# Projecting grouped q, k, v and memory's values with tokens on the rows, and a computed order for TensorE

## The chip, the cores and the metric

The kernel runs on one core of one Trainium2 chip. The metric is the device time of one execution in microseconds (us), the median of several runs. The core's engines are TensorE (PE; its weight loads are PEld), VectorE (DVE), ScalarE (ACT) and GpSimd (POOL); SyncE (SP) issues nearly all DMAs. 0.2% of the time before is 2.7 us.

## The reference

Two layers of an encoder over 512 tokens of width 1024, then a final RMSNorm. The token grid is 8 by 64; memory has 256 tokens.

```python
for l in range(2):
    h = rms_norm(x, norm_mix[l])
    na_q, na_k, na_v, g_q, g_k, g_v = split(h @ w_in[l])          # 512, 512, 512, 512, 128, 128 columns
    na = neighbourhood_attention(na_q, na_k, na_v, rpb)           # 8 heads of 64, a window of the grid
    g_q = rope(rms_norm_per_head(g_q)); g_k = rope(rms_norm_per_head(g_k))
    gqa = attention(g_q, g_k, g_v)                                # 8 q heads, 2 k/v heads, all 512 tokens
    x = x + concat(na, gqa) @ w_out[l]
    m = rms_norm(mem, norm_mem_kv[l])
    x = x + attention(rms_norm(x) @ w_mem_q, k(m), v(m)) @ w_mem_o   # 4 heads of 128
    u = conv3(rms_norm(x) @ w_up[l]) + conv_b                     # 2 x 2816 columns
    x = x + (silu(gate(u)) * val(u)) @ w_down[l]
return rms_norm(x)
```

## The kernel before

**Layout and precision.** x lies transposed, eight tiles `xT[c]` of 128 features by 512 tokens. Every float32 operand of a product is split into a rounded part `hi` and a rest `lo`, and a product is three matmuls, hi·hi, hi·lo and lo·hi, accumulated in PSUM (`mm3`; `gemm_T` runs it over chunks of 128 features). `Norm` holds the scaled operand (`xg`) and sums the squares.

**Weights.** `plan` lists the weight tiles in the order of use (`cols`, `plan_layer`, `plan_down`). `get_w` loads a tile through SP's queue into one of two `raw` buffers; `emit_split` (L647, L648) casts `hi` on ScalarE and subtracts `lo` on GpSimd (or VectorE), into one of four buffers. The last six tiles of the last down projection go into `r` tiles instead, which are held for both halves of the tokens.

**A layer.** Neighbourhood attention runs eight units (`na_scores` to `na_values`) woven with filler: `attn_fill` is a list of generators of projection work, a stretch of which is emitted between the steps of the units (`weave`, `NA_FILL`). The units project in `NA_ORDER`: q and k per pair of heads with the features on the rows (`project_qk`, 24 matmuls of 512 columns), v per four heads with the tokens on the rows, 256 columns at a time (`project_v`). The filler goes on with `gqa_project` in `GQA_ORDER`, out_na, the memory's keys and values (256 columns at a time) and the start of the output projection. Grouped attention follows in 16 units (`gqa_scores` to `gqa_values`), paced by `GQA_SLOT`.

**Grouped q, k, v before.** `gqa_project` makes one pair of heads, features on the rows, 512 tokens as columns. `gqa_rope` (L1255 to L1257) multiplies by the sine and cosine tables and squares; half-swapped rows are made by four DMAs; the sums of squares per head are four matmuls against `pairs` into a `tr` bank; k's inverse roots are spread over the rows by four matmuls against `ident`. `gqa_v` transposes v back with four TensorE transposes. Each step is put off by `late(n, ...)`, n times 3600 ns of TensorE time as the program counts it.

**Order.** The program is traced once; then `Order` plans the order of the instructions of ScalarE, VectorE and GpSimd with a model of their times (`due`, `run`), and fixes it by added dependencies. TensorE and SP keep the program's order (`InOrder.keep`, L69 and L82 are the lines of its wrappers, which all their instructions show).

**End.** `down_last` computes the last group of seven chunks for 256 tokens at a time, twice, and closes the final norm for each half (`Norm.stat`, `finish`).

Of the kernel before, what the change touches and what calls it, by code (L numbers as in the profile page):

```python
# [1 line left out]

# [29 lines left out]
GROUPS = [(0, 8), (8, 7), (15, 7)]  # L32
EPS = 1e-6
# [6 lines left out]
NA_ORDER = [("q", 0), ("k", 0), ("q", 1), ("k", 1), ("v", 0), ("q", 2), ("k", 2), ("q", 3), ("k", 3), ("v", 1)]  # L40
# [31 lines left out]
class Counted(InOrder):  # L72
# [4 lines left out]
    def matmul(self, out, lhsT, rhs, **k):  # L77
        n = 1
        for d in rhs.shape[1:]:
            n *= d  # L80
        self.ns += max(107.0, (n + 32) / 2.4)
        return self.keep(self.engine.matmul(out, lhsT, rhs, **k))  # L82


class Free:


    def __init__(self, engine):
        self.engine = engine

    def __getattr__(self, name):
        return getattr(self.engine, name)
# [110 lines left out]
ROUNDS = 16  # L203
# [102 lines left out]
class Order:  # L306

    FREE = ("ACT", "DVE", "POOL")  # L310

    def __init__(self, tc, kept):
# [10 lines left out]
        self.credit, best = {}, None  # L323
        for _ in range(ROUNDS):
            self.due()
            end, order, late = self.run()
            if best is None or end < best[0]:
                best = end, order
            for j, by in late:
                self.credit[j] = self.credit.get(j, 0.0) + by  # L330
# [80 lines left out]
    def run(self):  # L411
# [3 lines left out]
        ready, free_at = [0.0] * n, dict.fromkeys(HAND_OVER, 0.0)  # L415
# [9 lines left out]
        order, late, product = {e: [] for e in self.FREE}, [], None  # L425
# [3 lines left out]
        def earliest(j):  # L429
# [18 lines left out]
            return max(t, free_at[steps[j].engine])  # L448

        def choose(e):  # L450

            known = [(t, j) for j in open_[e] for t in [earliest(j)] if t is not None]
# [39 lines left out]
        def over_(s, t, end):  # L492

            for q in self.after[s.index]:
                need[q] -= 1
                begun = s.engine == "PE" == steps[q].engine or (s.index, q) in self.loose
                ready[q] = max(ready[q], t if begun else end + self.wait(s, steps[q]))
                if not need[q] and steps[q].engine in self.FREE:
# [7 lines left out]
        while len(issued) < n or moving:  # L506
            best = None
            for e in HAND_OVER:
                if e in self.FREE:
                    c = choose(e)  # L510
                elif at[e] < len(written[e]):
# [16 lines left out]
            if e in self.FREE:  # L528
                open_[e].remove(j)
                order[e].append(s)  # L530
            else:
                at[e] += 1
            if e == "PE":
                if product is not None and t > product + 150:
                    late.append((j, t - product))
# [9 lines left out]
            free_at[e] = t + s.busy  # L545
            issued.add(j)
            for name in s.names:
# [5 lines left out]
            if s.dma:  # L553
                if not moving:
                    clock = max(clock, t)
                moving.append([t + DMA_NS, s.bytes, j])
            else:
                over_(s, t, t + s.takes)
# [5 lines left out]
def encoder_kernel(ctx: ExitStack, tc: tile.TileContext, t: dict, out: bass.AP):  # L564
    nc = tc.nc
    kept = set()
    PE, SP = Counted(tc, nc.tensor, kept), InOrder(tc, nc.sync, kept)
# [65 lines left out]
    def emit_split(act=ACT, cuts=2):  # L633
# [6 lines left out]
        if eng[1:] == "r":  # L640
            hi, lo = rtile((nk, ncol)), rtile((nk, ncol))
        else:
            hi = wpool.tile([P, nk, ncol], F32R, tag="hi", name=nm("hi"))
            lo = wpool.tile([P, nk, ncol], F32R, tag="lo", name=nm("lo"))
# [6 lines left out]
    def get_w(key, ahead=AHEAD):  # L651
        n = done[0]
        assert plan[n][0] == key, (plan[n][0], key)
        ahead = n + 1 + ahead
        while ahead < min(len(plan), n + 1 + AHEAD_HELD) and plan[ahead][4][1:] == "r":
            ahead += 1
# [4 lines left out]
        while len(ready) < min(len(plan), ahead):  # L661
# [5 lines left out]
        else:  # L667
            load()
        done[0] += 1
# [12 lines left out]
    def plan_down(l, g):  # L682
        for m in range(KC):
            held = l + 1 == DEPTH and g + 1 == len(GROUPS) and m >= 2
            cols(("down", g, m), t["w_down"][l], *GROUPS[g], P * m, P, "Pr" if held else "P")

    def plan_memv(l, g):
        for kh in range(2):
            cols(("memv", g, kh), t["w_mem_kv"][l], 4 * kh, 4, 512 + 256 * g, 256)

    def plan_layer(l):
        w_in, w_out = t["w_in"][l], t["w_out"][l]
        for n, p in NA_ORDER:
# [6 lines left out]
        for n, g in enumerate(GQA_ORDER):  # L700
            c = {"k": 2048, "v": 2176}.get(g)
            cols(("g", g), w_in, 0, KC, 1536 + P * g if c is None else c, P)
        for mp in range(4):
            cols(("outn", mp), w_out, 0, 4, 256 * mp, 256, "P")
        for m in range(4):
            cols(("memk", m), t["w_mem_kv"][l], 0, KC, P * m, P)
        plan_memv(l, 0)
        for mp in range(4):
# [5 lines left out]
            if mp == 0:  # L714
                plan_memv(l, 1)
# [49 lines left out]
    qkg = cpool.tile([P, DEPTH, 2], F32, name="qkg")  # L765
# [4 lines left out]
    def load_parameters():  # L770
        SP.dma_start(par[:, 0, 8:], t["par"][:, 0, 8:])
        SP.dma_start(par[:, 1], t["par"][:, 1])
        SP.dma_start(qkg, t["qkg"])
# [4 lines left out]

    pairs = cpool.tile([P, 2], F32, name="pairs")
    nc.vector.memset(pairs, 0.0)  # L780
    for j in range(2):
        nc.vector.memset(pairs[64 * j : 64 * j + 64, j : j + 1], 1.0)
# [11 lines left out]
    def row_rep(rstd, n, tag, bufs, copy):  # L794

# [1017 lines left out]
```

## Time and profile before

| | |
|---|---|
| median of 3 runs | 1351.61 us (1350.64 to 1352.07) |
| the profiled execution | 1351.96 us |
| its span, first to last instruction | 1350.1 us |
| busy: PE, PEld, DVE, ACT, POOL | 1337.5, 1146.4, 902.1, 681.0, 698.8 us |
| instructions | 19133, of them 7018 matmuls |
| DMA | 139.88 MB, mean 104 GB/s |

Busy times of the engines overlap each other, and TensorE's overlap themselves: a matmul starts before its predecessor has drained, so a mean duration of one is longer than the step from one start to the next. A float32 matmul (against `ones`, `pairs`, `ident`) shows as two records. In rows of groups, the count stands behind x, and after the bar busy us, mean ns of one, and idle time of the engine before them with what ended it. The rows of waits give us in total, times, longest.

### The profile page before, as it was taken

The page shows a single profiled execution, that of the slowest core. Times are in us where ns is not written, and L with a number is a line of the kernel's source. Part 1 is how long each engine was busy: PE and PEld are TensorE (multiplying, and loading weights), DVE is VectorE, ACT ScalarE, POOL GpSimd, SP SyncE. Part 2 cuts the span into 40 slices and gives each one's busy share as a digit, 9 for nine tenths or more (in the row PEclk, how much of TensorE's full clock was granted, in tenths as well). Part 3 has the DMA queues.
Part 4 walks back from the last instruction along what each step waited for, and adds up shares of the span by engine and source line. Part 5 has one row for each costly group of instructions (what it writes and reads, how often), then busy time and mean ns, then how long its engine had stood idle before and what let it go on. Part 6 is the DMA issues. An engine that isn't in the chain of part 4 may idle for free.

```text
span 1350.1 us, 19133 instructions
## 1 busy us (share of the span) xinstructions
PE 1337.5 (99%) x7018; PEld 1146.4 (85%) x7018; DVE 902.1 (67%) x1598; ACT 681.0 (50%) x1258; POOL 698.8 (52%) x483
## 2 busy tenths in 40 slices
PE   9999999999999999999999999999999999999997
PEld 7898899888888888888898888988888888888887
DVE  6678874775984388178546678746769825862874
ACT  6776676564442244233557667855644423432441
POOL 2558766626444443443744576655554444444541
PEclk9999999999999999999999999999999999999999
DMA  7773222313333333332455531233233333333321
GB/s 217 201 190 109 79 63 73 116 45 96 96 103 98 94 94 94 109 94 82 127 155 164 140 106 49 79 95 94 63 94 98 104 94 94 93 95 109 90 83 63
DMA packets 219214, 139.88 MB, mean 104 GB/s; under 512 B 6000, under 2 KB 212080, under 8 KB 219120
## 3 DMA queue, kind: packets, MB, share of 16 engines
q1 hardware_dynamic: 218432, 138.13, 35.4%
q8 instruction: 56, 0.92, 0.3%
q10 hardware_dynamic: 688, 0.52, 0.1%
q14 instruction: 38, 0.31, 0.1%
HBM read 126.05 MB, written 2.10 MB: 95 GB/s over the span
## 4 chain that ended last, share of the span: by engine, by line
PE 93%; DVE 2%; DMA 1%; issue 1%; ACT 1%; POOL 1%; SPq 0%; DVEq 0%; POOLq 0%; ACTq 0%
PE mm L82 81%; PE sc L82 7%; PE tr L69 4%; PE tr L82 1%; DMA raw<-in_w_down 1%; POOL r L648 1%; DMA xT<-in_xT 0%; DVE t L846 0%; DMA raw<-in_w_in 0%; ACT r L1075 0%; SPq L69 0%; DVE r L875 0%; ACT hi L647 0%; ACT t L1257 0%; DVE r L1684 0%
## 5 line engine op out<-in xcount | busy, mean ns | idle before, releaser
L648 POOL TENSOR_TENSOR lo<-raw,hi 128x1024 fp32r<-128x1024 f32 (+2 forms) x268 | 511.5, 1919 | 498.6 <-ACT hi L647 494.7
L82 PE MATMUL mm<-xg,hi 128*128 128x512 f32 x1920 | 595.0, 391 | 0.0
L82 PEld LDWEIGHTS mm<-xg,hi 128*128 128x128 f32 x1920 | 356.1, 188 | 70.9
L647 ACT CAST hi<-raw 128x512 fp32r<-128x512 f32 (+2 forms) x276 | 226.3, 839 | 318.8 <-PE mm L82 267.8
L82 PE MATMUL mm<-xg,lo 128*128 128x512 f32 x960 | 373.9, 389 | 0.0
L82 PE MATMUL mm<-r,hi 128*128 128x512 f32 (+1 forms) x1096 | 316.3, 372 | 0.6 <-DVE r L1641 0.5
L1635 DVE SCALAR_TENSOR_TENSOR t<-t,par,t 128x7 f32<-128x7 f32 (+1 forms) x352 | 251.2, 773 | 25.0 <-ACT t L1628 25.0
L82 PEld LDWEIGHTS mm<-r,hi 128*128 128x128 f32 x1096 | 198.6, 189 | 35.6 <-DVE r L1641 0.7
L82 PEld LDWEIGHTS mm<-xg,lo 128*128 128x128 f32 x960 | 180.2, 188 | 37.9
L82 PE MATMUL mm<-r,lo 128*128 128x512 f32 (+1 forms) x548 | 203.6, 372 | 0.0
L82 PEld LDWEIGHTS mm<-r,lo 128*128 128x128 f32 x548 | 103.3, 188 | 17.9
L881 POOL TENSOR_SCALAR t<-t,s 128x512 f32<-128x512 f32 (+1 forms) x112 | 67.9, 622 | 75.0 <-DVE s L1323 36.1
L1620 DVE TENSOR_TENSOR t<-mm,rep 128x512 f32<-128x512 f32 x88 | 60.0, 686 | 63.0 <-PE mm L82 47.3
L1664 DVE TENSOR_TENSOR xT<-xT,mm 128x512 f32<-128x512 f32 x32 | 22.0, 686 | 104.5 <-PE mm L82 104.5
L1640 ACT CAST r<-t 128x512 fp32r<-128x512 f32 x44 | 27.3, 620 | 101.7 <-DVE t L1638 101.7
L1638 DVE TENSOR_TENSOR t<-t,t 128x512 f32<-128x512 f32 x44 | 68.2, 1551 | 4.3 <-ACT t L1637 0.5
L82 PE MATMUL sc<-r,r 128*128 128x256 f32 (+1 forms) x352 | 70.7, 333 | 0.3 <-DVE r L1081 0.3
L1628 ACT ACTIVATE t<-t,par 128x512 f32<-128x512 f32 x88 | 67.0, 806 | 1.2 <-DVE t L1620 1.2
L1317 ACT ACTIVATE t<-sc,s,qr 128x512 f32<-128x512 f32 x64 | 49.3, 775 | 32.2 <-DVE s L881 32.2
L82 PE MATMUL mm<-r,r 128*128 128x256 f32 (+1 forms) x428 | 62.5, 297 | 1.7 <-POOL r L648 1.1
L69 PE MATMUL tr<-ident,t 128*128 128x128 f32 x456 | 61.0, 273 | 0.7 <-DVE s L1267 0.7
L82 PEld LDWEIGHTS mm<-r,r 128*128 128x128 f32 x428 | 56.4, 191 | 5.0 <-POOL r L648 1.3
(160 smaller groups left out, 1607.8 us busy)
## 6 DMA issues: line engine op xcount, KB each, us to landing
raw<-in_w_up SPq DMA_DIRECT2D x88, 512.0 KB, 3.8
raw<-in_w_in SPq DMA_DIRECT2D x33, 512.0 KB, 4.1
raw<-in_w_down SPq DMA_DIRECT2D x32, 448.0 KB, 3.7
raw<-in_w_mem_kv SPq DMA_DIRECT2D x16, 512.0 KB, 3.8
raw<-in_w_down SPq DMA_DIRECT2D x16, 512.0 KB, 4.0
r<-in_bias SPq DMA_DIRECT2D x16, 384.0 KB, 4.9
r<-r SPq DMA_DIRECT2D x22, 256.0 KB, 5.6
raw<-in_w_out SPq DMA_DIRECT2D x8, 512.0 KB, 3.7
```

The lines of the kernel that those rows point to most:

```text
L69: return lambda *a, **k: self.keep(op(*a, **k))
L82: return self.keep(self.engine.matmul(out, lhsT, rhs, **k))
L647: act.copy(hi[:, k], raw[:, k])
L648: (POOL if eng[0] == "P" else DVE).tensor_sub(lo[:, k], raw[:, k], f(hi)[:, k])
L881: eng.tensor_scalar(e, e, sums[:, col : col + 1], 1.0, op0=ALU.mult, op1=ALU.mult)
L1317: ACT.activation(e, sc[j], AF.Exp, bias=nmx[:, c], scale=qrs[i][:, col : col + 1], accum_out=sums[:, c])
L1620: DVE.tensor_mul(u, us[side], ffn.rep)
L1628: ACT.activation(cc, u, AF.Identity, bias=par[:, l, CB + ch : CB + ch + 1], scale=w[1])
L1635: DVE.scalar_tensor_tensor(cc[:, dst], u[:, src], wi, cc[:, dst], op0=ALU.mult, op1=ALU.add)
L1638: DVE.tensor_mul(cs[0], cs[0], cs[1])
L1640: ACT.copy(acts[j][0], cs[0])
L1664: DVE.tensor_add(xT[m], xT[m], pm)
```

## The change

- Grouped q (`gq`) and grouped k and v together with the neighbourhood heads' second v (`kv`) are projected with the tokens on the rows, 512 columns of weights at a time, by `wide`; the memory's values too. `wide_cols` plans four weight tiles of two chunks by 512 columns for each.
- Rope is done with tokens on the rows: tables multiplied by the gains on GpSimd once a layer, the half swap as an addition of other columns on GpSimd, the sums of squares by VectorE reduces. The results are transposed by TensorE, four transposes per block of tokens for q and four for k. `gq` now holds blocks of tokens instead of pairs of heads.
- The filler's order changes: all grouped projections come in `NA_ORDER`, then the memory's values, out_na, two of the memory's keys; the other two keys go between the output rows.
- `Order` plans TensorE's order too, over the next 240 products that are not issued, replays each plan with spread times, and asks for 100 ns of margin at the operands that come from other engines.
- The last down group is split into four chunks for all 512 tokens and three chunks for each half; the final gain is applied on ScalarE, the last two squares are summed on TensorE, and the final multiplies take two chunks at a time.
- In layer 0's first k the second `lo` copy is made by GpSimd.

The diff, cut to its core:

```diff
-NA_ORDER = [("q", 0), ("k", 0), ("q", 1), ("k", 1), ("v", 0), ("q", 2), ("k", 2), ("q", 3), ("k", 3), ("v", 1)]
+NA_ORDER = [("q", 0), ("k", 0), ("q", 1), ("k", 1), ("v", 0), ("q", 2), ("k", 2), ("q", 3), ("k", 3), ("kv", 1), ("gq", 0)]
...
-GQA_ORDER = ["k", 0, 1, "v", 2, 3]
-NA_FILL = 2430
+NA_FILL = [[2800] * 6 + [1500] * 4, [2800] * 6 + [1400] * 4]
...
+TABLES = 1
 LATE = 3600
-N_RAW, N_W, N_R, N_T, N_S, AHEAD, AHEAD_HELD, N_WARM, N_LATE, N_FIRST = 2, 4, 21, 14, 24, 2, 5, 7, 4, (8, 16)
+N_RAW, N_W, N_R, N_T, N_S, AHEAD, N_WARM, N_FIRST = 2, 4, 21, 14, 24, 2, 7, (12, 24)
...
-class Counted(InOrder):
+class Free:
...
-        return self.keep(self.engine.matmul(out, lhsT, rhs, **k))
...
+        return self.engine.matmul(out, lhsT, rhs, **k)
...
+ROUNDS, REPLAYS, MARGIN, SHARES, STRETCH, SEED = 16, 2, 100.0, (0.0, 0.0, 0.5, 1.0, 2.0), 250, 0
+DMA_SPREAD = 1900.0, 3100.0
+AHEAD_MOST, PATIENCE = 240, 60.0
...
+    ORDERED = FREE + ("PE",)
...
+            for i in range(REPLAYS):
+                e, _, more = self.run(order, random.Random(i))
+                end, late = end + e, late + more
...
+        def product_next():
+            mine, i, seen, best = written["PE"], at["PE"], 0, None
+            while i < len(mine) and seen < AHEAD_MOST:
+                j = mine[i]
+                i += 1
+                if j in issued:
+                    continue
+                seen += 1
+                t = earliest(j)
+                if t is not None and (best is None or t < best[0] - PATIENCE):
+                    best = t, j
+                if best is not None and best[0] <= free_at["PE"] + PATIENCE:
+                    break
+            return best
...
+                short = MARGIN - (t - possible(j, fed))
+                if product is not None and short > 0:
+                    late.append((j, t - product, t - product + short))
...
-    PE, SP = Counted(tc, nc.tensor, kept), InOrder(tc, nc.sync, kept)
+    PE, SP = Counted(nc.tensor), InOrder(tc, nc.sync, kept)
...
+        if (l, g) == (DEPTH - 1, len(GROUPS) - 1):
+            for i, rows in enumerate(LAST):
+                for mp in range(4):
+                    cols(("down", "ab"[i], mp), t["w_down"][l], *rows, 256 * mp, 256)
+            return
         for m in range(KC):
-            held = l + 1 == DEPTH and g + 1 == len(GROUPS) and m >= 2
-            cols(("down", g, m), t["w_down"][l], *GROUPS[g], P * m, P, "Pr" if held else "P")
-    def plan_memv(l, g):
-        for kh in range(2):
-            cols(("memv", g, kh), t["w_mem_kv"][l], 4 * kh, 4, 512 + 256 * g, 256)
+            cols(("down", g, m), t["w_down"][l], *GROUPS[g], P * m, P)
...
+    def wide_cols(key, w, *slices):
+        for i in range(4):
+            loads, c = [], 0
+            for a, b in slices:
+                loads.append((lambda r, c=slice(c, c + b - a): r[:, :, c],
+                              w[2 * i * P : 2 * (i + 1) * P, a:b].rearrange("(k p) c -> p k c", p=P)))
+                c += b - a
+            plan.append(((key, i), loads, 2, 512, "P"))
...
+            elif n == "kv":
+                wide_cols(n, w_in, (1280, 1536), (2048, 2304))
+            elif n == "gq":
+                wide_cols(n, w_in, (1536, 2048))
...
+        wide_cols("memv", t["w_mem_kv"][l], (512, 1024))
...
-            DVE.tensor_scalar(part, sums(self.acc), 1.0 / D, EPS, op0=ALU.mult, op1=ALU.add)
-            warm()
-            DVE.scalar_tensor_tensor(v, sums(self.last), 1.0 / D, part, op0=ALU.mult, op1=ALU.add)
+            DVE.tensor_scalar(part, sums(self.acc, self.last[0]), 1.0 / D, EPS, op0=ALU.mult, op1=ALU.add)
+            DVE.scalar_tensor_tensor(v, sums(self.last[1]), 1.0 / D, part, op0=ALU.mult, op1=ALU.add)
...
-                    DVE.tensor_sub(k[o, 1], pm[r], f(k[r, 0]))
+                    POOL.tensor_copy(k[o, 1], k[r, 1])
...
+        def wide(key, blocks, ops, evict):
+            w, pms = [], {}
+            order = [(0, 0), (0, 1), (1, 0), (0, 2), (1, 1), (0, 3), (1, 2), (1, 3)]
+            order += [(b, i) for b in range(2, blocks) for i in range(4)]
+            for b, i in order:
+                if i == 0:
+                    pms[b] = ps_mm()
+                if i == len(w):
+                    w.append(get_w((key, i), min(AHEAD, N_W - 1 - i)))
+                bs = slice(b * P, b * P + P)
+                for k in (2 * i, 2 * i + 1):
+                    mm3(pms[b], ops[k][0][:, bs], ops[k][1][:, bs], *(v[:, k % 2] for v in w[i]), k == 0, k == KC - 1)
+                if b == blocks - 1 and i < AHEAD:
+                    prepare_w(i + 1)
+                if i == 3:
+                    evict(b, pms.pop(b))
+                yield
...
+        def project_kv(g):
+            vs = v_blocks(g)
+            gvt.append(rtile((NB, 2, P)))
+            gkt = [tmp() for _ in range(3)]
+            def evict(b, pm):
+                split_v(vblk[g][P * b], pm[:, 0:256], b)
+                split_v(gvt[0][:, b], pm[:, 384:512], b)
+                turn_by(1, pm[:, 256:384], b, *(v[:, b * P : b * P + P] for v in gkt))
+                if b == NB - 1:
+                    late(1, lambda: straddle(g, vs))
+                    late(1, lambda: gqa_k(*gkt))
+            yield from wide("kv", NB, xg, evict)
...
+        def gqa_tables():
+            rope, gains, tab = tmp((2 * NB, HD)), tmp((2, HD)), rtile((2, 2 * NB, HD), F32)
+            SP.dma_start(rope, t["rope"])
+            SP.dma_start(gains, t["qkg"][:, l])
+            for i in range(2):
+                POOL.tensor_tensor(tab[:, i], rope, gains[:, i].unsqueeze(1).to_broadcast([P, 2 * NB, HD]), op=ALU.mult)
+                gtab.append(tab[:, i].rearrange("p (t b) d -> p t b d", t=2))
...
-        def gqa_project(g):
...
+        def turn_by(i, pm, b, xs, cc, sq):
+            n = pm.shape[1] // HD
+            for v, tab in ((xs, gtab[i][:, 1, b]), (cc, gtab[i][:, 0, b])):
+                DVE.tensor_mul(by_head(v), by_head(pm), tab.unsqueeze(1).to_broadcast([P, n, HD]))
+            ACT.activation(sq, pm, AF.Square)
+        def rotate(xs, cc):
+            xs, cc = by_head(xs), by_head(cc)
+            halves = [slice(0, HD // 2), slice(HD // 2, HD)]
+            for a, b in (halves, halves[::-1]):
+                POOL.tensor_add(cc[:, :, a], cc[:, :, a], xs[:, :, b])
+        def transposed(cc):
+            tr = ps_t()
+            for c in range(4):
+                PE.transpose(tr[:, c * P : (c + 1) * P], cc[:, c * P : (c + 1) * P], ident)
+            return tr
...
+        def gqa_k(xs, cc, sq):
+            n = 2 * NB
+            ss, v, r = small(n), small(n), small(n)
+            DVE.tensor_reduce(ss, by_head(sq), axis=AX.X, op=ALU.add)
+            DVE.scalar_tensor_tensor(
+                v.rearrange("p (b j) -> p b j", j=2), ss.rearrange("p (b j) -> p b j", j=2), 1.0 / HD,
+                geps[:, 0].unsqueeze(2).to_broadcast([P, NB, 2]), op0=ALU.mult, op1=ALU.add)
+            POOL.tensor_tensor(r, v, mhalf[:, :n], op=ALU.pow)
+            rotate(xs, cc)
+            POOL.tensor_tensor(by_head(cc), by_head(cc), r.unsqueeze(2).to_broadcast([P, n, HD]), op=ALU.mult)
...
-        def gqa_rope(g, pm):
...
+        def project_gq():
+            yield from wide("gq", NB, xg, gqa_q)
+        def gqa_q(b, pm):
+            xs, cc, sq = tmp(), tmp(), tmp()
+            turn_by(0, pm, b, xs, cc, sq)
+            def norm():
+                ss, v = small(2 * NB), small(2 * NB)
+                DVE.tensor_reduce(ss, by_head(sq), axis=AX.X, op=ALU.add)
+                DVE.tensor_scalar(v, ss, geps[:, 1, b : b + 1], 1.0, op0=ALU.add, op1=ALU.mult)
+                POOL.tensor_tensor(qrs[b], v, mhalf[:, : 2 * NB], op=ALU.pow)
+                rotate(xs, cc)
+                late(1, turn)
+            def turn():
+                gq[b] = rtile((2, S))
+                split_q(transposed(cc), gq[b])
+            late(1, norm)
...
+            qs = slice(i * P, i * P + P)
+            assert gq[b] is not None and gk in whole_k
             sc = [ps_s() for _ in range(2)]
             for j in range(2):
                 for part in range(2):
-                    PE.matmul(sc[j], gq[i][:, j, qs], gk[j][:, part], start=part == 0, stop=part == 1)
+                    PE.matmul(sc[j], gq[b][:, j, qs], gk[j][:, part], start=part == 0, stop=part == 1)
...
+        def memory_values():
+            yield lambda: len(mops) == KC
+            memv.extend(rpair() for _ in range(MB))
+            yield from wide("memv", MB, mops, lambda b, pm: split_psum(*memv[b], pm, mem_rstd[:, b : b + 1]))
...
+        project = {"v": project_v, "kv": project_kv, "gq": lambda p: project_gq()}
...
-            PE, late, *([project_first(), *units[3:]] if l == 0 else units), *[gqa_project(g) for g in GQA_ORDER],
-            out_na(), memory_keys(), memory_values(0),
+            PE, late, *([project_first(), *units[3:]] if l == 0 else units),
+            memory_values(), out_na(), memory_keys(range(2)),
             close_rows(2, PartsView(parts, 4), lambda k: whole[k], lambda: nns.append(Norm(G_MQ, l)) or nns[0],
-                       memory_values(1)))
+                       memory_keys(range(2, 4))))
...
-            if s == 3:
-                gtab.append(rtile((2, S), F32))
-                SP.dma_start(gtab[0], t["rope"])
-                gqa_eps()
-            return [NA_FILL] * 3
+            if s == TABLES:
+                gqa_tables()
+            return [NA_FILL[l][s]] * 3
...
+        def down_last():
+            parts = [[acts.pop(j) for j in range(j0, j0 + nj)] for j0, nj in LAST]
+            ws = {}
+            def product(pm, i, m, ops):
+                if (i, m // 2) not in ws:
+                    ws[i, m // 2] = get_w(("down", "ab"[i], m // 2))
+                gemm_T(pm, ws[i, m // 2], ops, range(len(ops)), 0, len(ops) - 1, slice(P * (m % 2), P * (m % 2) + P))
+            for m in range(KC):
+                pm = ps_mm()
+                product(pm, 0, m, parts[0])
+                DVE.tensor_add(xT[m], xT[m], pm)
+            def finish(norm, y, last=False):
+                pr = row_bank(norm.rstd, NB // 2)
+                rep = tmp((256,))
+                ACT.copy(rep, (row_bank(norm.rstd, NB // 2) if last else pr)[:, :256])
+                for k in (0, 2, 6, 4):
+                    eng, by = (DVE, pr) if last and k < 6 else (POOL, rep)
+                    v = y[k // 4][:, k % 4 : k % 4 + 2]
+                    eng.tensor_mul(v, v, by[:, :256].unsqueeze(1).to_broadcast([P, 2, 256]))
+                for i, k in enumerate((0, 2, 4, 6)):
                     (ACT_IN_ORDER if last and i % 2 else SP).dma_start(
-                        out[k * P : (k + n) * P, norm.cols].rearrange("(k p) n -> p k n", p=P), y[k // 4][:, k % 4 : k % 4 + n])
-            norms = []
+                        out[k * P : (k + 2) * P, norm.cols].rearrange("(k p) n -> p k n", p=P), y[k // 4][:, k % 4 : k % 4 + 2])
+            norms, ys = [], []
             for half in range(2):
                 cs = slice(256 * half, 256 * half + 256)
-                hops = [(hi[:, cs], lo[:, cs]) for hi, lo in ops]
+                hops = [(hi[:, cs], lo[:, cs]) for hi, lo in parts[1]]
                 norms.append(Norm(cols=cs))
-                rows = []
+                ys.append([rtile((4, 256), F32) for _ in range(2)])
                 for m in range(KC):
-                    if half == 0:
-                        ws.append(get_w(("down", g, m)))
-                    rows.append(ps_mm()[:, :256])
-                    late = half == 0 and m < N_LATE
-                    gemm_T(rows[m], ws[m], hops, range(nj - 1 if late else nj), 0, nj - 1)
-                    for i in [m] if not late else range(N_LATE) if m == N_LATE - 1 else []:
-                        if late:
-                            gemm_T(rows[i], ws[i], hops, [nj - 1], 0, nj - 1)
-                        DVE.tensor_add(xT[i][:, cs], xT[i][:, cs], rows[i])
-                        norms[half].square(i)
-                        scale(half, i)
+                    pm = ps_mm()[:, :256]
+                    product(pm, 1, m, hops)
+                    DVE.tensor_add(xT[m][:, cs], xT[m][:, cs], pm)
+                    norms[half].square(m)
+                    ACT.activation(ys[half][m // 4][:, m % 4], xT[m][:, cs], AF.Copy, scale=gfin[:, m : m + 1])
```

More of the change, by code (lines that the diff above doesn't have):

```diff
@@ L447, in earliest @@
                 t = max(t, sorted(slots[k])[c - 1])
-            return max(t, free_at[steps[j].engine])
+            return t
+        def earliest(j):
+            t = possible(j, ready)
+            return t if t is None else max(t, free_at[steps[j].engine])
         def choose(e):
+            if given is not None:
+                if len(order[e]) == len(given[e]):
+                    return None
+                j = given[e][len(order[e])].index
+                t = earliest(j)
+                return None if t is None else (t, j)
             known = [(t, j) for j in open_[e] for t in [earliest(j)] if t is not None]
@@ L462, in choose @@
                     return t, q
-            return soon, j
+            if e == "POOL":
+                for q in open_["DVE"]:
+                    if steps[q].two_from_sbuf() and self.latest[q] < self.latest[j]:
+                        t = earliest(q)
+                        if t is not None and soon < t + 1 < soon + busy and soon + busy > self.latest[q]:
+                            t += steps[q].busy
+                            if t <= self.latest[j]:
+                                return max(t, soon), j
+            return soon, j
+        def product_next():
[6 more added lines that the diff above has]
+                seen += 1
+                t = earliest(j)
+                if t is not None and (best is None or t < best[0] - PATIENCE):
[3 more added lines that the diff above has]
+            return best
         def transfers(until):
@@ L497, in over_ @@
                 ready[q] = max(ready[q], t if begun else end + self.wait(s, steps[q]))
+                if s.engine != "PE":
+                    fed[q] = max(fed[q], end + self.wait(s, steps[q]))
                 if not need[q] and steps[q].engine in self.FREE:
@@ L544, in run @@
                 shared["DVE"] = t + s.busy
-            free_at[e] = t + s.busy
+            slow = 1.0 if draw is None or e not in self.FREE else 1.0 + 0.04 * draw.random()
+            free_at[e] = t + s.busy * slow
             issued.add(j)
+            while e == "PE" and at[e] < len(written[e]) and written[e][at[e]] in issued:
+                at[e] += 1
             for name in s.names:
@@ L639, in emit_split @@
             cuts = 1
[L640 to L644, printed above, removed]
+        hi = wpool.tile([P, nk, ncol], F32R, tag="hi", name=nm("hi"))
+        lo = wpool.tile([P, nk, ncol], F32R, tag="lo", name=nm("lo"))
         for i in range(cuts):
@@ L649, in emit_split, with prepare_w @@
         ready.append((hi, lo))
[L651 to L656, printed above, removed]
+    def prepare_w(ahead):
         def load():
@@ L850, in stat, with sums @@
             nb = self.n // P
-            def sums(sq):
+            def sums(*sqs):
                 pv = ps_t()
                 for b in range(nb):
-                    PE.matmul(pv[:, b : b + 1], sq[:, b * P : b * P + P], ones, start=True, stop=True)
+                    for i, sq in enumerate(sqs):
+                        PE.matmul(pv[:, b : b + 1], sq[:, b * P : b * P + P], ones, start=i == 0, stop=i == len(sqs) - 1)
                 return pv[:, 0:nb]
-            if self.last is None:
+            if not self.last:
                 self.rstd, self.var = rsqrt(sums(self.acc), nb, 1.0 / D, factor)
@@ L1793 @@
         "rope": _rope_tables(),
[L1794 removed]
+        "qkg": np.tile(np.stack([a[n][:, order] for n in ("gqa_q_norm", "gqa_k_norm")], axis=1), (P, 1, 1, 1)),
     }
```

240 lines of the change are left out of this document (82 added, 158 removed).

## The prediction

> **What bounds the kernel now.** I read the page first (busy shares, chain), then the chain in order of time, then TensorE's groups with shapes kept apart, then its waits, and last the windows of the attention stages.
>
> ```profile
> span 1350.1 us, 19133 instructions
> PE 1337.5 (99%) x7018; PEld 1146.4 (85%) x7018; DVE 902.1 (67%) x1598; ACT 681.0 (50%) x1258; POOL 698.8 (52%) x483
> PEclk9999999999999999999999999999999999999999
> PE 93%; DVE 2%; DMA 1%; issue 1%; ACT 1%; POOL 1%; SPq 0%; DVEq 0%; POOLq 0%; ACTq 0%
> ```
>
> TensorE is on 93% of the chain at full clock; the next engine, VectorE, is busy 67%. But a busy PE may still be stretched by short waits, so I price its work by the steps between starts. Two stretches of the chain have nothing but one shape:
>
> ```profile
> 328.00 342.76 PE mm L82 x1512
> 1330.01 10.07 PE mm L82 x84
> ```
>
> The first is layer 0's feed-forward part, all 512 columns: 342.76 / 1512 = 0.2267 us a matmul. The second is the end of the kernel, 256 columns: 10.07 / 84 = 0.1199 us. Two halves therefore cost 13.1 ns more than one whole. The small forms come from the order of time: eight transposes 83.82 to 84.65, so 0.104 each; eight records on `pairs` (four matmuls, two records each) 100.06 to 100.87, 0.81; eight on `ident,t` 110.05 to 110.94, 0.89.
>
> ```profile
> 83.82 1.07 PE L69 MATMUL tr<-ident,t 128*128 128x128 f32 x8
> 84.65 0.36 PE L82 MATMUL mm<-hi,xg 128*128 128x256 f32 x1
> ...
> 100.06 0.95 PE L82 MATMUL tr<-pairs,t 128*128 128x2 f32 x8
> 100.87 0.37 PE L82 MATMUL mm<-r,r 128*128 128x256 f32 x1
> ...
> 110.05 1.14 PE L82 MATMUL mm<-ident,t 128*128 128x128 f32 x8
> 110.94 0.48 PE L82 MATMUL mm<-xg,hi 128*128 128x512 f32 x1
> ...
> 164.82 1.17 PE L82 MATMUL sc<-r,r 128*128 128x512 f32 x4
> 165.82 0.64 PE L82 MATMUL mm<-xg,r 128*128 128x256 f32 x4
> ```
>
> The last pair shows a stall that no wait is listed for: four 512-column score products take 1.00 us, not 4 x 0.2267 = 0.91. About 0.09 us goes where a product's operand has only just come.
>
> Groups by shape (count, then busy and mean; busy overlaps, so I use the counts; first and last row of each width):
>
> ```profile
> L82 PE MATMUL mm<-xg,hi 128*128 128x512 f32 x1920 | 595.0, 391 | 0.0
> ...
> L69 PE MATMUL tr<-ident,t 128*128 128x128 f32 x456 | 61.0, 273 | 0.7 <-DVE s L1267 0.7
> L82 PE MATMUL mm<-r,r 128*128 128x256 f32 x380 | 49.5, 284 | 1.6 <-POOL r L648 1.1 <-ACT t L1257 0.5
> ...
> L82 PE MATMUL mm<-lo,r 128*128 128x256 f32 x64 | 18.1, 283 | 0.0
> ...
> L82 PE MATMUL sc<-xg,lo 128*128 128x512 f32 x32 | 12.3, 390 | 0.0
> L82 PE MATMUL tr<-pairs,t 128*128 128x2 f32 x80 | 9.5, 240 | 0.0
> L82 PE MATMUL tr<-ones,t 128*128 128x1 f32 x64 | 7.8, 241 | 0.2 <-DVE t L846 0.2
> ...
> L82 PE MATMUL mm<-ident,t 128*128 128x128 f32 x16 | 2.2, 280 | 0.0
> ```
>
> The ten 512-column groups hold 4616 matmuls (x 0.2267 = 1046.4), the nine of 256 columns 1712 (205.3), the transposes 47.4, `pairs` and `ones` some 15, the other small ones about 6: 1320 us of work. The span less about 4.5 us ahead of the first product and 6.7 us behind the last is 1339. So about 19 us of TensorE's time is stalls, and everything else is work: what the change takes off the work comes off the time, unless a new wait takes its place.
>
> ```profile
> PE mm L82 <- POOL r L648: 1.1, 1, 1.1
> PE mm L82 <- DVE r L1096: 0.7, 1, 0.7
> PE tr L69 <- DVE s L1267: 0.7, 1, 0.7
> PE mm L82 <- ACT t L1257: 0.5, 1, 0.5
> PE mm L82 <- DVE r L1641: 0.5, 1, 0.5
> PE sc L82 <- DVE r L1081: 0.3, 1, 0.3
> ```
>
> **The change, part by part** (TensorE's time over both layers).
>
> *Rope's sums.* The sums of squares per head no longer run on TensorE against `pairs`; VectorE reduces with tokens on the rows. Five projections a layer, ten groups of 0.81: -8.1 us. This is the largest term. The k rows spread through `ident` go too: two groups of 0.89, -1.8.
>
> *Transposes.* Grouped q needs four per block of tokens (16 a layer), k still 4 as new ones, and v's 4 go: 16 more a layer, 32 x 0.104 = +3.3.
>
> *Merged columns.* Values of heads 4-7 (96 halves a layer) together with grouped k and v (48 wholes) become 96 wholes: 48 merges a layer. Memory's values, 96 halves, become 48 wholes: 48 merges. The last down group, 336 halves, becomes 96 wholes and 144 halves: 96 merges. 288 x 13.1 ns = -3.8. The skill's page "TensorE: Matmul & The Clock Gate" (Back-to-back issue gap) speaks against this term: it gives the isolated gap as columns / 2.4 plus 2.5 ns, by which a merge is worth 2.5 ns, and the Trainium skill's sum for the 288 would be an estimated -0.7. The two stretches of one shape quoted above differ by 13.1 ns in this very kernel, so the trace disagrees and I stay with -3.8.
>
> *Closing sums.* In the last norm the sums of two squares are added on TensorE: four more small records in the first half, at about 0.1 each +0.4; the second half's lie under VectorE's work on the last row.
>
> Work in sum: -8.1 - 1.8 + 3.3 - 3.8 + 0.4 = **-10.0**.
>
> *The last down group* split 4 + 3. Its first products need the activations of columns 15-18 only, so the wait for the last one (L1641, 0.5) is covered by 8 x 12 x 0.2267 = 21.8 us, and the weights pass the ordinary buffers, at 5.4 us of products a tile, instead of six held ones (L648, 1.1). With 0.1-0.17 us of restart at each: **-2.1**. Late next is none: the last tiles' lo parts have the 5.4 us each.
>
> *The tail.*
>
> ```profile
> 1341.99 0.71 POOL s L867
> 1342.74 0.72 PE tr L82 x4
> 1343.46 0.02 issue
> ...
> 1343.56 0.38 ACT rep L801
> 1343.94 0.02 issue
> 1343.97 0.42 DVE r L1684
> ```
>
> VectorE's final multiplies stand behind ScalarE's copy of the same bank. With a second bank for the copy they can start near 1343.5; three pieces of 512 columns take as long as six of 256. **-0.4**, bounded by 0 (GpSimd's part ends last) and -0.5 (1343.97 to 1343.46).
>
> *Start.* For layer 0's first k, GpSimd copies what VectorE subtracted twice (L1081, L1096), and TensorE gets four more pieces of filler ahead of the first scores: of 0.7 + 0.3 and two restarts I take **-1.0**.
>
> *Moved to other engines.* Costed at nothing on TensorE's path, hidden by this slack:
>
> ```profile
> 100.00:130.00 30.00, 30.00 (x177) 26.24 (x177) 25.02 (x51) 20.49 (x51) 24.46 (x22) 1.00 0.38 109
> ...
> 175.00:215.00 40.00, 40.00 (x298) 37.33 (x297) 30.04 (x73) 31.17 (x73) 26.23 (x31) 1.00 0.22 66
> ```
>
> (columns: window, length, then PE, PEld, DVE, ACT, POOL busy.) VectorE per layer: five reduces come, close to this one's 682 ns, the subtractions of q get cheaper since they read PSUM, k's and v's multiplies go, four small pairs for kv come: about +1 us. GpSimd:
>
> ```profile
> L1278 POOL TENSOR_TENSOR t<-t,t 128x512 f32<-128x512 f32 x10 | 14.3, 1428 | 0.0
> L1272 POOL TENSOR_TENSOR qr<-s,mhalf 128x8 f32<-128x8 f32 x8 | 14.3, 1784 | 1.6 <-DVE s L1267 1.6
> ...
> L1314 DVE TENSOR_REDUCE s<-sc 128x1 f32<-128x512 f32 x64 | 42.0, 682 | 1.7 <-PE sc L82 1.5
> ```
>
> two table products and k's scaling at 1.43 each, less a copy, +4 us a layer; rotation in halves and powers as before. GpSimd's idle time in the 30 us shown is 5.5, so without that cover the weights' lo parts come up to 4 us late a layer.
>
> *SP's queue.* The four row-swap DMAs behind each rope go.
>
> ```profile
> SPq L69 <- DVE t L1255: 58.6, 10, 9.7
> ```
>
> SP stood 58.6 us behind them, weight loads queued after it; no PE wait names a load there, so I take 0. The tables' loads move from step 3 to step 1 of neighbourhood attention; the queue has weights and biases ahead of them, nothing waits for the tables before the first kv block. 0, bounded by -1 and +1.
>
> *TensorE's order computed.* Of 19.2 us of stalls, 2.1 and 1.0 are counted above, the tail's and the start's fixed part is about 3, leaving some 13, mostly restarts of 0.09. A product whose operand is not there can now be passed by a later one, and a product's feeders get 100 ns of margin. The wait on L1267 (0.7 and its restart) goes in any case with the `pairs` bank. But the order is planned on modelled times, and a bad guess is a new wait in a fixed order. Between -10 and +5, nearest the rows that name their cause, I take **-3.0**.
>
> Sum: -10.0 - 2.1 - 0.4 - 1.0 - 3.0 = -16.5; span 1350.1 to 1333.6. The profiled execution took 1351.96, 1.9 over its span; the runs' median 1351.61 is 0.35 below it. So 1333.6 + 1.86 - 0.35 = **1335.1**.
>
> **The rivals.**
>
> *The order takes nearly all of the stalls* (-10 instead of -3): 1328. For it: most are restarts a margin of 100 ns is meant for. Against: the restarts at the scores follow VectorE's and ScalarE's chains, which stay.
>
> *The order gains nothing*, and L1641 or L648 has a successor: 1335.1 + 3 to 5 = 1339.
>
> *The saved time turns into waits on other engines* in neighbourhood attention, where grouped q, k and v now all have to be projected. GpSimd at 24.46 of 30 speaks for it, ScalarE and VectorE at 78% and 75% in the window from 175 against. Then some 4.5 us a layer come back: 1344.
>
> *Slower: the door to grouped attention.* Before, its first scores needed one pair of q heads and k; two q projections came as filler later. Now its first four units need all four blocks of q, and k. From a block's last product: two multiplies and a reduce (2.1), the power (1.8), rotation (1.5), two deferrals of 3.6, transposes and splits (an estimate of 3 from two such multiplies and their ScalarE partners): about 15 us, covered by memory's values (48 x 0.2267 = 10.9) and three units. If that cover is used up too early, TensorE idles once a layer. At 9.6 us a layer (1335.1 + 19.2 = 1354.3) it decides for slower; the most, 15 uncovered, gives 1365.
>
> *No change*: a wait of 8 us a layer at the same door, 1351.
>
> **How the numbers follow.** Forecast (1331-1339) 0.50; order takes nearly all (below 1331) 0.16; order gains nothing (1339-1342) 0.14; waits on other engines (1342-1348.9) 0.08; no change 0.06; slower 0.06. 0.2% is 2.7 us, about what this measurement can tell from no change. Faster 0.88, same 0.06, slower 0.06. Range for eight in ten: 1327 to 1344, cutting 0.06 below and 0.14 above. The likeliest case's own is 1331 to 1339.
>
> **What would show it.** `tr<-pairs` gone; 512-column matmuls at 4616 plus 288, 256-column ones at 1712 less 576; the transposes at 488; no PE wait for a held weight near the end; score quartets of 1.00 us rarer. Wrong would be: TensorE's idle time in one piece of over 5 us ahead of the first four-product score units of grouped attention, or GpSimd's weight subtractions named as releasers between 40 and 140 us; or stalls above 19 us in all, spread thin, which would be the computed order.

## The result and the profile after

The changed kernel takes 1340.88 us (median of 4 runs, 1340.48 to 1341.53); the ratio to the kernel before is 0.9923 (95% interval 0.991 to 0.9937). The kernel before has 1351.34 with one run more. Forecast were 1335.1 with a range of 1327 to 1344: the direction and the range held, but the gain came to 10.5 us where 16.5 had been forecast, and the time lies outside the likeliest case's own 1331 to 1339, in the bracket of "the order gains nothing".

The page after:

```profile
span 1338.9 us, 18447 instructions
PE 1329.0 (99%) x6672; PEld 1123.0 (84%) x6672; DVE 888.4 (66%) x1590; ACT 686.5 (51%) x1282; POOL 710.2 (53%) x504
PEclk9999999999999999999999999999999999999999
PE 93%; DVE 2%; ACT 2%; DMA 1%; issue 1%; POOL 0%; SPq 0%; POOLq 0%; DVEq 0%; ACTq 0%
```

By shares nothing has changed: TensorE is still 99% busy and 93% of the chain. TensorE's groups by shape (first and last row of the new 512-column products, the sums against `ones`, and the transposes of grouped q and k):

```profile
L95 PE MATMUL mm<-hi,xg 128*128 128x512 f32 x256 | 87.4, 397 | 0.0
...
L95 PE MATMUL mm<-lo,r 128*128 128x512 f32 x32 | 12.6, 399 | 0.0
...
L95 PE MATMUL tr<-ones,t 128*128 128x1 f32 x72 | 8.8, 243 | 0.2
...
L1367 PE MATMUL tr<-ident,t 128*128 128x128 f32 x40 | 6.1, 275 | 0.0
```

The rows on `pairs` are gone, and the counts are those forecast: 4904 matmuls of 512 columns, 1136 of 256, 488 transposes. TensorE's waits after (us in total, times, longest):

```profile
PE tr L95 <- POOL ident masks.py:199: 1.3, 1, 1.3
PE sc L95 <- ACT t L1430: 1.0, 1, 1.0
PE tr L1297 <- DVE r L1170: 0.9, 2, 0.7
PE mm L95 <- DVE t L967: 0.3, 2, 0.2
PE tr L95 <- POOL s L944: 0.3, 1, 0.3
PE sc L95 <- ACT xg L72: 0.2, 1, 0.2
```

The waits on the held weights and on the last activation are gone, and those at layer 0's first scores. New are L1430 (an exponential of grouped attention ahead of the second unit's scores in layer 1) and L1170 (VectorE's splitting of a transposed q block, ahead of transposes of the neighbourhood heads).

To keep work and waits apart I took every matmul's start from the trace: the step to the next start less the step of its shape (227 ns for 512 columns, 120 for 256, 109 for 128, 112 for one or two) is a stall where it is over 6 ns. The rest of TensorE's stretch from first start to last end is work:

| profiled execution | span | first start to last end | stalls | work |
|---|---|---|---|---|
| before | 1350.1 | 1342.1 | 20.8 | 1321.3 |
| after | 1338.9 | 1332.1 | 21.2 | 1311.0 |
| program_order | 1349.4 | 1341.8 | 30.1 | 1311.7 |
| before_planner | 1349.4 | 1341.4 | 20.3 | 1321.1 |
| seed1 | 1340.5 | 1333.3 | 22.3 | 1311.0 |
| rounds48 | 1338.5 | 1331.3 | 20.4 | 1310.9 |
| old_end | 1341.4 | 1333.1 | 21.9 | 1311.2 |
| ballast | 1351.1 | 1343.9 | 24.3 | 1319.6 |
| up_halves | 1353.4 | 1346.6 | 22.2 | 1324.4 |
| q_bank | 1346.2 | 1339.5 | 27.9 | 1311.6 |
| q_bank_program | 1356.3 | 1349.1 | 36.9 | 1312.2 |
| fill3000 | 1343.5 | 1336.0 | 25.1 | 1310.9 |
| early_prepare | 1342.0 | 1334.6 | 23.7 | 1310.9 |
| margin300 | 1341.9 | 1334.4 | 23.3 | 1311.1 |

The work column hardly moves within one arrangement (1310.9 to 1312.2), so the reading holds. From before to after: work -10.3, stalls +0.4, and -1.3 at the two ends, outside TensorE's stretch. (These are spans of one execution each; they differ by 11.2 us, the medians by 10.5.) Two signs named in the prediction came out against it: stalls are 21.2 us (20.8 before), over the 19 named there, and steps of over 280 ns between two score products of 512 columns are no rarer, 32 before and 32 after.

### The profile page after: what moved, and what is told of

It reads as the page before. It is cut to its first block, busy times and chain, and to the rows that moved or that the text cites. A ratio compares the mean times of both kernels' runs of the same rounds, so it can differ in the third digit from the quotient of the medians.

```text
span 1338.9 us, 18447 instructions
## 1 busy us (share of the span) xinstructions
PE 1329.0 (99%) x6672; PEld 1123.0 (84%) x6672; DVE 888.4 (66%) x1590; ACT 686.5 (51%) x1282; POOL 710.2 (53%) x504
## 4 chain that ended last, share of the span: by engine, by line
PE 93%; DVE 2%; ACT 2%; DMA 1%; issue 1%; POOL 0%; SPq 0%; POOLq 0%; DVEq 0%; ACTq 0%
PE mm L95 83%; PE sc L95 6%; PE tr L1451 2%; PE tr L95 1%; DMA xT<-in_xT 1%; PE tr L1297 1%; PE tr L1634 1%; DVE t L923 0%; ACT t L1275 0%; DVE r L1170 0%; DVE sc L1269 0%; ACT r L951 0%; ACT t L1321 0%; DVE r L952 0%; SPq L72 0%
## 5 line engine op out<-in xcount | busy, mean ns | idle before, releaser
L714 POOL TENSOR_TENSOR lo<-raw,hi 128x512 fp32r<-128x512 f32 (+3 forms) x278 | 529.0, 1911 | 518.1 <-ACT hi L713 512.3
L95 PE MATMUL mm<-xg,hi 128*128 128x512 f32 x1728 | 533.4, 390 | 0.0
L713 ACT CAST hi<-raw 128x512 fp32r<-128x512 f32 (+3 forms) x282 | 232.7, 843 | 336.8 <-PE mm L95 283.7
L95 PEld LDWEIGHTS mm<-xg,hi 128*128 128x128 f32 x1728 | 322.5, 188 | 65.5
L95 PE MATMUL mm<-r,hi 128*128 128x512 f32 (+1 forms) x1200 | 343.3, 370 | 0.3 <-DVE t L967 0.3
L95 PE MATMUL mm<-xg,lo 128*128 128x512 f32 x864 | 336.3, 389 | 0.0
L95 PE MATMUL mm<-r,lo 128*128 128x512 f32 (+1 forms) x600 | 221.7, 370 | 0.1
L95 PEld LDWEIGHTS mm<-xg,lo 128*128 128x128 f32 x864 | 162.2, 188 | 34.1
L95 PE MATMUL mm<-hi,xg 128*128 128x512 f32 (+1 forms) x384 | 111.0, 359 | 0.0
L958 POOL TENSOR_SCALAR t<-t,s 128x512 f32<-128x512 f32 (+1 forms) x112 | 66.5, 607 | 51.8 <-DVE s L1281 23.3
L95 PEld LDWEIGHTS mm<-hi,xg 128*128 128x128 f32 x384 | 68.3, 189 | 9.0 <-DVE r L1170 0.2
L95 PE MATMUL mm<-lo,xg 128*128 128x512 f32 (+1 forms) x192 | 68.9, 359 | 0.0
L1430 ACT ACTIVATE t<-sc,s,qr 128x512 f32<-128x512 f32 x64 | 49.3, 776 | 32.5 <-DVE s L958 32.4
```

Source lines behind the costliest of these rows:

```text
L95: return self.engine.matmul(out, lhsT, rhs, **k)
L713: act.copy(hi[:, k], raw[:, k])
L714: (POOL if eng[0] == "P" else DVE).tensor_sub(lo[:, k], raw[:, k], f(hi)[:, k])
L958: eng.tensor_scalar(e, e, sums[:, col : col + 1], 1.0, op0=ALU.mult, op1=ALU.mult)
L1430: ACT.activation(e, sc[j], AF.Exp, bias=nmx[:, c], scale=qrs[b][:, col : col + 1], accum_out=sums[:, c])
```

## The experiments

Unless said otherwise the edits are to the changed kernel, and medians stand against its 1340.9.

**program_order and before_planner: the two halves of the change apart.**

```diff
-AHEAD_MOST, PATIENCE = 240, 60.0
+AHEAD_MOST, PATIENCE = 1, 60.0
```

> The changed kernel, with the planner's look-ahead for TensorE cut to the next product (AHEAD_MOST = 1), so that TensorE keeps the program's order while all else of the change stays. Theory A (the computed order gains little, since TensorE's stalls are 21 us after and 21 us before): 1340.9 plus 0 to 3. Theory B (the computed order itself makes the new waits of some 5 us in the attention stages): 1336 to 1339. Theory C (the new project-first arrangement makes large waits and the order hides most of them): over 1346, with TensorE's idle time in pieces of over 1 us around the start of grouped attention.

Measured: 1351.6, ratio to before 1.0002 (0.9993 to 1.0011). All of the gain is gone. Its longest waits:

```profile
PE tr L1297 <- DVE r L1170: 4.0, 2, 3.7
PE mm L95 <- DVE t L967: 2.1, 2, 1.1
PE mm L95 <- POOL lo L714: 1.5, 4, 0.6
...
PE tr L1367 <- DVE r L952: 1.0, 2, 0.6
```

The 10 us of work saved are there, and 9 us of stalls more than in the changed kernel. Theory C holds. before_planner is the kernel before with the new class `Order` and `PE, SP = Counted(nc.tensor), InOrder(tc, nc.sync, kept)` alone.

> The kernel before with only the new planner (TensorE's order computed, replays, margin); the projections, the sums against pairs and the last group are as before. Theory A: 1351 less 0 to 2. Theory B (the computed order hurts by itself): over 1352.5. Theory C (the order is worth much wherever operands come late): 1343 to 1347, most of it from the waits of 1.1, 0.7, 0.7, 0.5, 0.5 and 0.3 us that the profile before lists.

Measured: 1350.7, ratio 0.9996 (0.9987 to 1.0005): not to be told from none, as theory A had it. On the old arrangement the order exchanged the listed waits for others (5.0 us in all against 5.8) and left the stalls as they were, 20.3 us against 20.8. So neither half shows a gain alone: medians of -0.6 for the order and +0.3 for the rest, both within the noise, and -10.5 together. (In both runs the new `Order` also plans the other engines.)

**seed1, rounds48 and margin300: how much is chance of the plan.**

```diff
-ROUNDS, REPLAYS, MARGIN, SHARES, STRETCH, SEED = 16, 2, 100.0, (0.0, 0.0, 0.5, 1.0, 2.0), 250, 0
+ the same line, in seed1 with SEED 1, in rounds48 with ROUNDS 48, in margin300 with MARGIN 300.0
```

> The changed kernel with the planner's random seed 1 instead of 0: another plan of the same work. All theories: TensorE's instructions are the same in number, so the time moves only by stalls. If plans of equal worth differ by less than 1 us, differences of 2 us between the other kernels mean something; if this one moves by 2 us or more, the place of the new waits is chance of the plan and not of the change.

> The changed kernel with 48 instead of 16 rounds of planning. If the planner's search is what leaves the 21 us of stalls: 1337 to 1339.5. If the rest is restarts of 0.09 us after operands that no order brings earlier: 1340.9 within 0.7.

> The changed kernel with the planner asking for 300 instead of 100 ns between a product's operands from other engines and its start. If the restarts of 0.09 us (some 9.5 us in sum) come from operands that a plan could bring earlier: 1336 to 1339 and score quartets of 1.00 us rarer. If they follow from chains that no order shortens (the second scores wait for the exponentials of the unit before): 1340.9 within 1, quartets as many.

Measured: 1341.1, 1341.0 and 1343.1 (ratios to before 0.9925, 0.9923, 0.994). Another seed moves the median by less than 1 us, and a longer search finds nothing. A larger margin costs 2.2 us, which neither case had, and four-product scores restart as often (34 steps over 0.28 us between two such products, 32 with 100 ns). So asking the planner for more margin does not take the restarts away; that they come from chains that no order shortens fits this and is not shown by it.

**old_end: the last group, norm and multiplies as before.** `down_last`, `Norm` and the last group's `plan_down` with its six held tiles were put back; the computed order stays.

> The changed kernel with the last down group, the last norm's sums and the final multiplies as before. If the end is worth what the two profiles show (96 merged columns 1.25, two waits with restarts 2.1, tail 6.66 to 5.41 = 1.25, less 0.8 for more sums): 1340.9 + 3.8 = 1344.7. If the planner of TensorE's order covers the waits of the old end too: 1342.6. If the tail is bound by the last DMA in any form: 1343.5.

Measured: 1343.7, so the end is worth 2.8 us, between the first and the second expectation. The number is nearest the third, whose condition does not hold, since the tail did change. In spans, work differs by 0.2 (merged columns against added sums and a second bank), stalls by 0.7, and the stretch behind TensorE's last matmul is 7.0 instead of 5.4; counted from the closing sums against `ones`, 10.5 instead of 9.8, the rest being a later last matmul. The held weights cost 0.5 us of wait here, 1.1 in the kernel before.

**ballast: is TensorE's work worth its time?**

```diff
+        def ballast():
+            pv = ps_t()
+            for b in range(NB):
+                PE.matmul(pv[:, 2 * b : 2 * b + 2], ident, ident[:, 0:2], start=True, stop=True)
```

called once in each `gqa_q` and behind the last block of `project_kv`.

> The changed kernel with the ten groups of four small float32 matmuls put back (against ident instead of pairs, two columns each, results unused), one at each grouped projection. Theory A (what leaves TensorE's work leaves the time one to one): 1340.9 + 10 x 0.81 = 1349.0. Theory B (the work in the attention stages is partly hidden behind waits for other engines): 1340.9 plus 2 to 5, with fewer stalls.

Measured: 1353.6, ratio 1.0024 (1.0015 to 1.0033). Work +8.6, near the 8.1 expected; in addition stalls +3.1, with one wait of 2.7 us (last entry) in layer 0, at the scores of grouped attention's third unit; L1437 here is the changed kernel's L1430:

```profile
PE sc L95 <- ACT t L1437: 3.7, 2, 2.7
```

Theory B falls: nothing of this work was hidden. The time rose by 12.8 us, more than theory A's 8.1: the groups also made stalls where they stand, which I had not priced. Each takes a `tr` bank as well; whether the bank or TensorE's time makes these stalls is not separated.

**up_halves: what a merge is worth.**

```diff
+            for h in range(2):
+                c = slice(256 * h, 256 * h + 256)
+                gemm_T(pm[:, c], w, [(hi[:, c], lo[:, c]) for hi, lo in ffn.ops], range(KC), 0, KC - 1)
```

for layer 0's `up_project`.

> The changed kernel with layer 0's up projections (all but those of chunk 0: 42 x 24 = 1008 products) done in two halves of 256 columns instead of 512, to measure what a merge is worth. By the steps of the two one-shape stretches, 13.1 ns each: 1340.9 + 13.2 = 1354.1. By the isolated gap of the Trainium skill's page TensorE: Matmul & The Clock Gate (2.5 ns each): an estimated 1343.4.

Measured: 1355.7, +14.8 for 1008 halvings. By the table 13.4 us of this is work, 13.3 ns a halving (mean steps of 120.0 ns for 256 columns and 226.7 for 512 in layer 0's feed-forward part); stalls rose by 1.0. The chain's stretch of that part, after and here:

```profile
324.83 341.13 PE mm L95 x1505
```

```profile
324.00 355.90 PE mm L95 x2496
```

The stretch is 14.8 us longer too, though it does not begin at the same product. The Trainium skill's isolated gap ("TensorE: Matmul & The Clock Gate", Back-to-back issue gap) does not hold for this stream of weight load and product; the steps of the trace do.

**q_bank_program and q_bank: which banks are short?**

```diff
         def transposed(cc):
-            tr = ps_t()
+            tr = ps_mm()
```

> TensorE in the program's order (look-ahead 1), and the transposes of grouped q and k into one of the four mm banks instead of one of the two tr banks. If the two tr banks, which each transpose holds until two ScalarE and two VectorE instructions have split it, make the waits that the fixed order shows (3.7 + 0.3 us at the q transposes, 1.0 us at the transposes of the neighbourhood heads): 1351.6 - 5 = 1346.6. If VectorE is late as such, and any bank would do: 1351.6 within 1.5, with the waits at other lines.

> The changed kernel, TensorE's order computed, with the transposes of grouped q and k into an mm bank. If the tr banks hold up the computed order too (waits of 0.7 + 0.2 us at the q transposes, with restarts 1.2): 1339.5. If the order has already passed what can be passed: 1340.9 within 0.7. If the projections need all four mm banks: over 1342.

Measured: 1358.1 (6.5 over program_order) and 1347.9 (7.0 over the changed kernel). For q_bank_program I had it the wrong way round; q_bank met its third case. The waits move to the mm banks, at the square of a wide projection (L1356) and the split of a k (L1153), here in q_bank_program:

```profile
PE mm L95 <- ACT t L1356: 5.7, 4, 2.5
PE mm L95 <- DVE r L1153: 4.1, 4, 1.7
```

The four mm banks are needed by the wide projections, whose banks now stay occupied for VectorE's two multiplies and ScalarE's square.

**early_prepare and fill3000: is the start of grouped attention crowded, or late?**

```diff
-            if s >= 5:
+            if s >= 3:
                 prepare.step(1)
```

```diff
-NA_FILL = [[2800] * 6 + [1500] * 4, [2800] * 6 + [1400] * 4]
+NA_FILL = [[3000] * 6 + [1500] * 4, [3000] * 6 + [1400] * 4]
```

> The changed kernel with the memory's operands prepared from step 3 of neighbourhood attention instead of step 5, so that their eight ScalarE and eight VectorE instructions lie ahead of the start of grouped attention. If VectorE's and ScalarE's crowding there makes the waits of 0.7 (transposes of grouped q) and 1.0 us (first scores) in layer 1: 1338.5 to 1340, and these two waits shorter. If the waits come from the chain from the last q block itself: 1340.9 within 0.7.

> The changed kernel with 3000 instead of 2800 ns of filler between the first six steps of neighbourhood attention (3.6 us of projections more ahead of grouped attention in all), so that the last q block is done earlier. If the start of grouped attention waits for that block's chain: 1339 to 1340, the wait of 1.0 us at the first scores gone. If the waits only move: 1340.9 within 1.

Measured: 1343.1 and 1344.6, both slower; neither expectation. The waits named are shorter or gone, and others take more than their place: in early_prepare L1323 (1.3 us, VectorE's last addition of a neighbourhood unit) and L714 (0.8, GpSimd's part of a weight), in fill3000 L952 (1.8) and L1153 (1.5), both VectorE's subtractions. By steps, the place aimed at did gain a little: stalls from 765 to 830 us, around layer 1's start of grouped attention, fell from 5.3 to 4.4 and 4.3. But both edits act in layer 0 too, and there, from 38.5 to 150 us, stalls rose from 3.1 to 5.7 and 6.5; the longest is fill3000's on L1153 at 71 us. The windows show how full the engines are. Before, then after, each over 765:780, 780:795 and 795:810, the stretch in which layer 1 goes over to grouped attention (columns: window, length, PE, PEld, DVE, ACT, POOL busy, clock, DMA share, GB/s):

```profile
765.00:780.00 15.00, 14.34 (x88) 12.55 (x87) 9.83 (x26) 9.35 (x24) 10.20 (x11) 1.00 0.36 101
780.00:795.00 15.00, 14.49 (x80) 12.36 (x79) 10.49 (x21) 7.79 (x17) 10.32 (x8) 1.00 0.46 124
795.00:810.00 15.00, 15.00 (x82) 12.65 (x81) 12.73 (x27) 11.64 (x26) 12.92 (x12) 1.00 0.37 103
```

```profile
765.00:780.00 15.00, 14.96 (x93) 13.00 (x93) 14.28 (x34) 10.67 (x26) 12.49 (x16) 1.00 0.50 127
780.00:795.00 15.00, 14.27 (x80) 11.41 (x80) 13.83 (x31) 12.61 (x31) 8.93 (x11) 1.00 0.09 26
795.00:810.00 15.00, 13.99 (x69) 11.14 (x67) 13.94 (x28) 10.79 (x24) 12.46 (x12) 1.00 0.35 115
```

VectorE was busy 33.1 of 45 us and is busy 42.1 of 45 now, 93% (before, its fullest 45 us there, 795 to 840, had 37.9), though over the whole span it has less to do (888.4 against 902.1 us). Grouped projections that were spread into grouped attention as filler now come in one piece ahead of it, with the heads' own work and the memory's operands. ScalarE rose as well, from 28.8 to 34.1. In layer 0 the windows from 105 to 150 us give another picture: VectorE 39.2 before and 40.1 after, ScalarE 29.4 and 35.7. That VectorE's crowding makes the waits is read from layer 1's windows and the names of the releasers; a run with VectorE or ScalarE unloaded there was not made, so it is not shown by an experiment, and ScalarE's part stays open.

## Why the prediction was right or wrong

*Bound and work (-10.0): right.* TensorE's work fell by 10.3. A merge measures 13.3 ns of work where 13.1 were set, and the sums against `pairs`, put back, 8.6 us where 8.1 were set.

*Last group (-2.1): right in the profile.* Stalls from 1290 us to the last products fell from 2.3 to 0.2. In old_end, with the old end and the computed order, they are 0.9, so the order alone has most of it.

*Start (-1.0): right.* The stalls between 24 and 38.5 us fell from 1.7 to 0.5; in before_planner they are 1.4, in program_order 0.5, so it is not the order that took them.

*Tail (-0.4): right.* Behind the last product TensorE goes on to the sums against `ones`; before and after:

```profile
1339.92 0.50 PE L82 MATMUL tr<-ones,t 128*128 128x1 f32 x4
```

```profile
1329.07 1.71 PE L95 MATMUL tr<-ones,t 128*128 128x1 f32 x12
...
1332.65 1.88 DVE L1790 TENSOR_TENSOR r<-r,tr 128x512 f32<-128x512 f32 x3 [1.68 <-PE tr L95]
1333.51 0.37 ACT L1786 COPY t<-tr 128x256 f32<-128x256 f32 x1 [3.00 <-PE tr L95]
```

From there to the span's end it was 10.2 us and is 9.8, and VectorE starts ahead of ScalarE's copy. The 1.3 us at the ends above are mostly a shift of the mark, since TensorE's last matmul now makes the copy's own bank.

*TensorE's order (-3.0) and the moved work at nothing: the steps that failed.* I set the order against the old stalls and took the new arrangement as free. Between 38.5 and 1290 us the stalls rose from 13.0 to 16.4, +3.4 instead of -3.0, and that is the miss. They rose around the starts of grouped attention, whose first scores stand at 136 and 790 us: from 1.1 to 2.6 between 100 and 150 us and from 3.0 to 5.3 between 765 and 830. In program_order the stalls between 38.5 and 1290 us are 25.6: the new arrangement makes 12.6 us of them (1.7 behind one wait, at a lower clock), more than the work it saves, and the computed order takes 9.2 back. On the old arrangement the order's worth is not to be told from none. So the sign "stalls above 19 us in all" came, but not from the computed order, to which the prediction would have put it. The range held although this term had the wrong sign, because it reached up to 1344 for the rivals. "VectorE about +1 us a layer, hidden by this slack" had the sum too high (up to 1290 us VectorE's busy time fell from 866.7 to 863.2) and the place wrong: I read the slack from windows of the old arrangement in which the moved work did not lie. Which engine's queue makes the new waits is, as said above, not shown.

*The rivals.* "The order gains nothing" comes nearest in the number, partly by luck: its condition, a successor of the waits at the last group, is not what happened, and on this arrangement the order is worth 10.7 us (program_order against the changed kernel). The door to grouped attention was near the right place: in the program's order TensorE waits 3.7 us in one piece there. But it is not the first scores that wait for the chain of the last q block; it is transposes of the neighbourhood heads, for VectorE's split of a transposed q block (L1170), and the computed order leaves waits of 0.7 and 1.0. The rival of other engines eating the saved time came true for program_order, where 9.6 us of work go and stalls rise by 9.3, and for some 3.4 us of the kernel as it is.

## What to carry to other kernels

On an engine that is 99% busy, count its work by steps from start to start: the work saved comes off the time, and the stalls stand as a sum of their own that a new arrangement can fill up again. When work is moved to an engine with slack, look for the slack in the stretch where the work will stand, with everything else that moves there, not over the layer; and when an edit aims at one stretch, sum the stalls of the other stretches too, since here the other layer lost more than the place aimed at gained. A computed order and an arrangement that needs one have to be judged together: apart, neither of these showed a gain.

## What the runs showed that I had not expected

A single wait of 3.7 us costs more than its length. In program_order the granted clock falls to half behind it, and the products behind it lose another 1.7 us by their steps:

```profile
787.00:791.50 4.50, 0.92 (x9) 0.68 (x7) 4.32 (x11) 4.39 (x12) 1.40 (x2) 1.00 0.00 0
791.50:793.00 1.50, 1.42 (x7) 1.25 (x8) 1.23 (x3) 1.45 (x5) 0.58 (x2) 0.73 0.00 0
793.00:795.00 2.00, 2.00 (x6) 1.54 (x6) 1.80 (x4) 1.20 (x4) 0.81 (x2) 0.50 0.00 0
795.00:797.00 2.00, 2.00 (x12) 1.73 (x11) 0.39 (x1) 1.79 (x4) 1.58 (x2) 0.85 0.00 0
```

Between 793 and 795 us products start 0.43 us apart, at a clock of 0.50, where at full clock they take 0.227. The page "TensorE: Matmul & The Clock Gate" of the Trainium skill (What's actually happening) gives half rate after an idle window of about 3.4 us; this trace agrees. Behind ballast's wait of 2.7 us the clock stays at 1.00 in the window from 153 to 156.
